# Fifteen gate pairs and two plain tiles, with the operand work moved ahead

## The chip, the cores and the metric

The kernel runs on one core of one Trainium2 chip. The metric is the device time of one execution in microseconds (us), as the median of several runs. One execution was also recorded by the hardware profiler; all rows shown below are from such a recording. Engines are named as in the profile: PE (TensorE matmuls), PEld (its weight loads), DVE (VectorE), ACT (ScalarE), POOL (GpSimd), SP (SyncE). SPq is SP's queue of DMA issues.

## The reference

One layer of a hybrid backbone is run for 512 latent tokens and for 128 context tokens. The kernel holds them together as 640 columns (T = 640). After a norm and a modulation the layer input h (1024 features) goes through one projection into four branches: a gated convolution (a), a bidirectional linear recurrence (b), attention (c), and a chunked gated MLP (d). Each branch gives an output y of 256 features. The four are joined under gates and projected, and a second half (norm, a convolutional feed-forward block) follows:

```python
g_a, g_b, g_c, g_d = jnp.split(jax.nn.sigmoid(h @ lw['w_gate'] + lw['b_gate']), N_BRANCH, axis=-1)
merged = (g_a * (y_a @ lw['w_br_a']) + g_b * (y_b @ lw['w_br_b'])
          + g_c * (y_c @ lw['w_br_c']) + g_d * (y_d @ lw['w_br_d']))
return merged @ lw['w_o'], kh, vh, s_f, s_b
```

The change lies in the stage that computes `merged`: for each of four branches, eight output tiles of 128 features, each a gate product (1024 features deep) and a branch product (256 deep).

## The kernel before

**Precision.** Every operand of a large product is kept as two parts: a high part (ACT copies it into the rounded type) and a low part (DVE subtracts the high part from the original). A product of a block takes three matmuls: high by high, high by low, low by high. All matmuls of this stage are 128 by 128 by 320; the 640 columns are two halves of 320 (HC = 320).

**Plain tiles.** `gate_tile` computes one output tile directly: 2 halves, 8 blocks of h, 3 matmuls each (line 375), then a sigmoid on ACT (line 1003), then 2 halves, 2 blocks of y, 3 matmuls each, then a product on DVE into `merged` (line 1014). For the plain tiles of branch d the low part of the weights is made by an ACT copy with scale -1 (line 151) and an accumulating DMA from POOL (`low_dma`).

**Pairs.** Two output tiles n and n + 4 of a branch form a pair. Weights and columns are cut in two by two blocks, and the pair is computed with seven block products in place of eight (`gprod` for h, line 1186; `bprod` for y, line 1195). Each of the seven takes 4 blocks of h and 1 of y, with 3 matmuls each. The price is sums and differences of blocks:

- of h, made once: three differences on DVE (line 1051), one sum (line 1071), and the high and low parts of the results (`g_split`, lines 1077 and 1078). Operands 7, 5 and 6 go to the regions F, X1 and X0; operand 3 is written over the block (0, 1) of h itself, in the tiles XH and XL. The generator `g_operands` does this while attention and the last projections run.
- of y, made once per branch: the plain y is loaded into the tile D (`y_load`: a DMA from SP for the high part, then an accumulating DMA from POOL for the low part), four sums on DVE (`y_sums`), and copies into the region C, and into y itself (`y_split`).
- of the weights, made for each pair: raw weights (two loads, line 1122; the second of an odd pair goes to region G), four sums (`g_s01`, `g_s23`), and the units A, B, C and Z (Z in region S0) with high and low parts (`g_a`, `g_al`, `g_b`, `g_c`, `g_zh`, `g_zl`). The units A, B, C take in turn the three places of the pool `w`, which the plain tiles use too, and every fourth unit takes region B.

The list `PAIRS` starts in branch d at n = NPL. With NPL = 2 the tiles 0, 1, 4, 5 of branch d are plain and fourteen pairs follow. `g_first` prepares pair 0; `g_all` runs the pairs. `g_pair` writes one pair: products 1, 2, 6, 5, 7, 4, 3, with the copies, sigmoids and weight units of the next pair written between them. Products 1, 6, 7 and 4 add up in one accumulator, b1; ACT copies it between (to `ga`, then `gb`).

**Order of the work.** A scheduler orders the instructions of each engine by its own simulation of when they are ready, with those that were written earlier first. `keep_in_program_order` pins an instruction behind the one that was written last on its engine. The wrappers `oact`, `ovec`, `opool` do that for every call while `fixed[0]` is true, which holds from the start of the pairs in `g_all`. Before that they are plain calls. `act` and `vec` in this part of the kernel are always plain.

Generators such as `g_operands` and `attn` are jobs: a running count of TensorE time, `now`, advances with the matmuls that are written, and a job is resumed when its next due time is reached (`yield 2` means 2 us later). `R` holds flags: "scores" is set one step after attention has written its last score products, "ya" when the convolution branch's y is split (line 676), "yc" when attention's y is written, "ada39" when the last of the early modulation columns is done; `drain` resumes jobs until a condition holds.

Of the kernel before, what the change touches and what calls it, by code (L numbers as in the profile page):

```python
# [9 lines left out]
F32 = mybir.dt.float32  # L10
F32R = mybir.dt.float32r
U8 = mybir.dt.uint8
AF = mybir.ActivationFunctionType
ALU = mybir.AluOpType
AX = mybir.AxisListType

P = 128
# [25 lines left out]
""".split()  # L43
WARM = 100
UE = [5, 3, 1]
NPL = 2
LOWD = ("ac", "ax", "ab", "d")
T = 640
TS = 512
HC = 320  # L50
# [20 lines left out]
def tile_step(ctx: ExitStack, tc: tile.TileContext, a: dict, outs: list, dbg=None):  # L71
    nc = tc.nc
# [7 lines left out]
    gp = ctx.enter_context(tc.tile_pool(name="gp", bufs=4))  # L80
# [15 lines left out]
    def step(j):  # L96
        try:
            j[0] = now[0] + (next(j[1]) or 0.0) * j[2]
        except StopIteration:
            jobs.remove(j)  # L100
# [14 lines left out]
    def drain(done):  # L115
        busy[0] = True
        while not done():
            assert jobs
            for j in list(jobs):
                step(j)  # L120
            now[0] += 1.0
        busy[0] = False
# [3 lines left out]
    def nm(s):  # L126
        cnt[0] += 1
        return f"{s}_{cnt[0]}"

    def region(tag, shape, dt=F32):  # L130
        return big.tile(shape, dt, tag=tag, name=nm(tag))
# [23 lines left out]
    ten, vec, pool = [Ordered(e, boot) for e in (nc.tensor, nc.vector, nc.gpsimd)]  # L155
    act, mm = Ordered(nc.scalar, boot).activation, ten.matmul
    ovec, opool, oact = Ordered(nc.vector), Ordered(nc.gpsimd), Ordered(nc.scalar).activation
# [51 lines left out]
    for x in LORD.split():  # L209
        if x[0] == "w":  # L210
            i, h = int(x[1]), int(x[2])
# [180 lines left out]
    R = {}  # L392
# [567 lines left out]
    for s in SECTIONS:  # L960
        for n in range(2):
            if s in TOK:
                plain(lambda s=s, n=n: rows(a["w_tok"][TOK.index(s), n], 4, 256),
                      lambda w, s=s, n=n: tok_tile(s, n, w))
            else:
                plain(lambda s=s, n=n: feat(a["w_in"][OFF[s] // P + n], dma=s in LOWD),
                      lambda w, s=s, n=n: in_tile(s, n, w))

    hdr = dram.tile([2, 2, P, 4, HC], F32, name="hdr")
# [19 lines left out]
    GI = dict(a=0, b=1, c=2, d=3)  # L989
    PAIRS = [(0, n) for n in range(NPL, 4)] + [(bi, n) for bi in range(1, 4) for n in range(4)]  # L990
    GPAIR = len(PAIRS)
# [44 lines left out]
    gx, gw = {}, {}  # L1036

    def g_operands():
        while "cg" not in R:
            yield 1  # L1040
        d, g = region("D", [P, 2, 4, HC]), region("G", [P, 4, HC])
        yield 8
        for x, h, c in ((d[:, 0], 0, 1), (d[:, 1], 1, 1), (g, 0, 0)):
            yield 10
            nc.sync.dma_start(x, hdr[h, c])
        while "ya" not in R:
            yield 1
        yield 5
        a21, a22, a11 = d[:, 0], d[:, 1], g
        for o, x, y in ((a22, a21, a22), (a21, a11, a21), (a11, a22, a11)):  # L1050
            tc.keep_in_program_order(vec.tensor_tensor(o, x, y, ALU.subtract))
            yield 2
        gx["x"] = {}
        for i, h, c in ((1, 0, 0), (2, 1, 0), (4, 1, 1), (3, 0, 1)):
            cs = slice(c * HC, (c + 1) * HC)
            gx["x"][i] = xh[:, 4 * h:4 * h + 4, cs], xl[h][:, :, cs]
        for i, x, t, key in ((7, a21, "F", "scores"), (5, a22, "X1", "yc"), (6, a11, "X0", "yc")):
            while key not in R:
                yield 1
            y = region(t, [P, 2, 4, HC], F32R)  # L1060
            gx["x"][i] = y[:, 0], y[:, 1]
            g_split(i, x)
            if i == 5:
                nc.sync.dma_start(a22, hdr[1, 0])
            yield 1.5
        gx["t3"] = a22, a11
        gx["Y"] = a21.rearrange("p a t -> p (a t)")
        gx["S"] = a22.rearrange("p a t -> p (a t)").rearrange("p (i k c) -> p i k c", i=2, k=5)
        y_load(0)
        yield 7  # L1070
        vec.tensor_tensor(a22, a22, a11, ALU.add)
        y_sums()
        R["gx3"] = True

    def g_split(i, x):
        h, l = gx["x"][i]
        act(h, x, AF.Copy)
        vec.tensor_tensor(l, x, h.bitcast(F32), ALU.subtract)

    def y_load(bi):  # L1080

        if bi < 2:
            h, l = [R["y" + BR[bi]][:, i].rearrange("p k t -> p (k t)").bitcast(F32) for i in range(2)]
        else:
            h, l = [(ybd if bi == 2 else ycd)[:, i].rearrange("p k t -> p (k t)") for i in range(2)]
        nc.sync.dma_start(gx["Y"], h)
        opool.dma_start(gx["Y"], l, accum_op=ALU.add)
# [25 lines left out]
    def gp_id(p_):  # L1113
        return PAIRS[p_]
# [16 lines left out]
    def low(w, x, h):  # L1131
        ovec.tensor_tensor(w, x, h.bitcast(F32), ALU.subtract)
# [5 lines left out]
    def g_al(p_, r):  # L1138
        w = gw[p_, "A"]
        low(w[:, 1], r[0], w[:, 0])  # L1140

    def g_s01(p_, r):

        s = gw[p_, "S"] = gx["S"] if p_ else region("G", [P, 2, 5, P])
        ovec.tensor_tensor(s[:, 0], r[0][:, 0], r[1][:, 1], ALU.add)
        ovec.tensor_tensor(s[:, 1], s[:, 0], r[1][:, 0], ALU.add)

    def g_s23(p_, r):
        s = gw[p_, "S"]
        b21, (b22, b12) = r[0][:, 1], (r[1][:, 0], r[1][:, 1])  # L1150
        ovec.tensor_tensor(b12, b12, b22, ALU.add)
        ovec.tensor_tensor(b21, s[:, 1], b21, ALU.add)

    def g_b(p_):
        s = gw[p_, "S"]
        b = gw[p_, "B"] = gunit(p_, 1)
        oact(b[:, 0], s, AF.Copy)
        low(b[:, 1], s, b[:, 0])

    def g_c(p_, r):  # L1160
        c = gw[p_, "C"] = gunit(p_, 2)
# [74 lines left out]
    def g_pair(p_, r):  # L1236
# [7 lines left out]
        bi, n0 = gp_id(p_)  # L1244
        new = n0 == (NPL if bi == 0 else 0)
        if new:
            gx["bi"] = bi
        if n0 == (NPL if bi == 0 else 0) + 1 and bi < 3:
            y_load(bi + 1)
# [68 lines left out]
        gprod(b2, p_, 3, False)  # L1318
        if n0 == (NPL if bi == 0 else 0) + 1 and bi < 3:
            y_sums()  # L1320
# [6 lines left out]
    def g_first(r):  # L1327
        drain(lambda: "ada39" in R)
        g_a(0, r[0])
        g_al(0, r[0])  # L1330
        g_s01(0, r[0])
        g_s23(0, r[0])
        g_b(0)
        for x in g_c(0, r[0]):
            low(*x)
        g_zh(0, r[0])
        return r

    def g_all(r):
        drain(lambda: "gx3" in R)  # L1340
        r[1] = gp_load(1)
        gx["C"] = region("C", [P, 2, 3, HC], F32R)
        fixed[0] = True
        sums_ = down_sums()
        for p_ in range(GPAIR + 1):
            for _ in range(4 if p_ else 0):
                next(sums_, None)
            if p_ == GPAIR:
                fixed[0] = False
                for j in range(GATES + 1, GATES + 3):  # L1350
                    ld[j] = units[j][0]()
                    rd[j] = units[j][1](ld[j])
            g_pair(p_, r)
        m_split(2)
        m_split(3)
# [1066 lines left out]
    for tok in BOOT:  # L2422
        name, on_act = tok.rstrip("."), tok[-1] == "."
        p = re.fullmatch(r"(m)(\d)(\d)([HL]+)|(tu|xo|sc|wh|wl)(\d)([ab])|([a-z]+)(\d+)|(\w+)", name).groups()
# [27 lines left out]
    ten, vec, pool, act, mm = nc.tensor, nc.vector, nc.gpsimd, nc.scalar.activation, nc.tensor.matmul  # L2452
# [111 lines left out]
```

## Time and profile before

| what | value |
|---|---|
| median of 3 runs | 1002.12 us (1001.3 to 1003.15) |
| the profiled execution's own time | 1001.64 us |
| its span, first to last instruction | 999.9 us |
| granted TensorE clock, mean | 0.998 of full speed |
| plain gate tiles in the trace | about 271.5 to 309.25 us |
| the fourteen pairs | 309.25 us to about 525 us |

A timeline row gives start (us), duration (us), engine, line, operation, out<-in by the program's names, shapes and count, and in brackets how long the engine was idle before it and what released it. Line 151 is the line of the wrapper, so instructions of the ordered calls are told apart by their tiles: `w`, `B`, `S` are weight units, `D` is y and the sums of weights, `C` the split sums of y, `ga` and `gb` the two gates of a pair, `F`, `X`, `XH`, `XL` the operands of h. On such rows a group of instructions of one kind is one row with its count. A row of the chain gives start, duration and engine with line. A row of DMA issues gives the queue, the size and the median time from issue to landing.

### The profile page before, as it was taken

The numbers are of one execution on the slowest core, as the hardware profiler recorded it, in microseconds if no ns is written. First come the engines' busy times: TensorE is split into PE (matmuls) and PEld (weight loads), VectorE is DVE, ScalarE is ACT, GpSimd is POOL, SyncE is SP. The second block draws the span as 40 slices with busy tenths as digits, with TensorE's granted clock in tenths as the row PEclk, the third lists the DMA queues.
The fourth block names the chain that finished last, engine by engine and source line by source line (L and its number), as shares of the span: only waits on it lengthen the run. The fifth ranks groups of instructions, "written<-read, shape, count | busy, mean of one in ns | idle before, by whom it ended". The sixth has DMA issues, their size and how long they took to land.

```text
span 999.9 us, 18964 instructions
## 1 busy us (share of the span) xinstructions
PE 987.3 (99%) x7467; PEld 935.7 (94%) x7467; DVE 860.6 (86%) x1411; ACT 585.3 (59%) x1009; POOL 169.9 (17%) x227
## 2 busy tenths in 40 slices
PE   8999999999999999999999999999999999999997
PEld 6899999999999999999998799999999999888886
DVE  6678899878677989898879978999999998999796
ACT  6642343445555565555655376777777777756672
POOL 1000020323110223233010021222222222100004
PEclk9999999999999999999999999999999999999999
DMA  9874343498475999999348785766666666976842
GB/s 357 331 252 155 123 143 119 132 251 255 107 212 188 309 235 237 291 257 293 106 163 319 296 316 161 216 161 173 177 168 163 177 171 192 365 257 226 283 127 105
DMA packets 71016, 214.16 MB, mean 214 GB/s; under 512 B 9744, under 2 KB 24880, under 8 KB 68240
## 3 DMA queue, kind: packets, MB, share of 16 engines
q1 hardware_dynamic: 43968, 151.22, 43.2%
q0 software_dynamic: 26960, 61.75, 26.8%
q8 instruction: 58, 0.95, 0.4%
q14 instruction: 30, 0.25, 0.1%
HBM read 168.62 MB, written 48.51 MB: 217 GB/s over the span
## 4 chain that ended last, share of the span: by engine, by line
PE 89%; DVE 5%; DMA 3%; issue 2%; POOL 1%; SPq 0%; ACT 0%; POOLq 0%; DVEq 0%; ACTq 0%
PE g L1622 21%; PE m L1186 17%; PE g L375 16%; PE m L2094 9%; PE m L1622 5%; PE g L2094 4%; PE g L1195 3%; PE g L948 2%; PE m L1392 1%; PE m L1195 1%; PE m L539 1%; PE m L1617 1%; DMA S<-in_w_ada_dram 1%; DMA B<-in_w_ada_dram 1%; PE g L151 1%
## 5 line engine op out<-in xcount | busy, mean ns | idle before, releaser
L375 PE MATMUL g<-XH,w 128*128 128x320 f32 x704 | 169.4, 316 | 0.0
L375 PEld LDWEIGHTS g<-XH,w 128*128 128x128 f32 x704 | 120.3, 188 | 2.5 <-issue 1.2
L375 PE MATMUL g<-XL,w 128*128 128x320 f32 x352 | 108.7, 309 | 0.0
L1186 PE MATMUL m<-XH,w 128*128 128x320 f32 x336 | 79.8, 309 | 0.0
L375 PEld LDWEIGHTS g<-XL,w 128*128 128x128 f32 x352 | 66.3, 188 | 0.0
L2094 PE MATMUL m<-w,XH 128*128 128x512 f32 x246 | 58.5, 390 | 0.0
L1186 PEld LDWEIGHTS m<-XH,w 128*128 128x128 f32 x336 | 57.6, 188 | 0.0
L2094 PEld LDWEIGHTS m<-w,XH 128*128 128x128 f32 x246 | 46.1, 188 | 9.5
L1186 PE MATMUL m<-XL,w 128*128 128x320 f32 x168 | 51.9, 309 | 0.0
L151 ACT ACTIVATE w<-raw 128x640 fp32r<-128x640 f32 (+3 forms) x53 | 49.6, 952 | 3.2 <-PE g L375 2.0
L151 DVE TENSOR_TENSOR w<-raw,w 128x640 fp32r<-128x640 f32 (+3 forms) x43 | 43.9, 1039 | 1.9 <-ACT w L151 1.9
L151 POOL DMA_DIRECT2D wsum<-in_w_dn_dram x36 | 37.4, 1256 | 44.6 <-issue 40.6
L1186 PE MATMUL m<-X,w 128*128 128x320 f32 x264 | 42.6, 309 | 0.0
L1186 PEld LDWEIGHTS m<-X,w 128*128 128x128 f32 x264 | 39.7, 188 | 0.0
L151 DVE SCALAR_TENSOR_TENSOR X<-MG,p2t,X 128x641 f32<-128x641 f32 x44 | 38.9, 883 | 0.9 <-ACT X L151 0.2
L151 DVE SCALAR_TENSOR_TENSOR X<-X,p2t,X 128x641 f32<-128x641 f32 x44 | 38.9, 884 | 0.9
L1622 PE MATMUL g<-XL,w 128*128 128x320 f32 x240 | 38.6, 310 | 0.0
L1622 PE MATMUL g<-XL,C 128*128 128x320 f32 x240 | 38.3, 309 | 0.0
L151 ACT ACTIVATE gb<-m 128x320 f32<-128x320 f32 x28 | 12.3, 438 | 43.0 <-PE m L1186 43.0
L1622 PEld LDWEIGHTS g<-XL,w 128*128 128x128 f32 x240 | 36.0, 188 | 0.6 <-ACT MG L151 0.3
L1622 PEld LDWEIGHTS g<-XL,C 128*128 128x128 f32 x240 | 36.0, 188 | 0.0
L1186 PEld LDWEIGHTS m<-XL,w 128*128 128x128 f32 x168 | 31.5, 188 | 0.0
(612 smaller groups left out, 2852.0 us busy)
## 6 DMA issues: line engine op xcount, KB each, us to landing
wsum<-in_w_dn_dram POOLq DMA_DIRECT2D x30, 512.0 KB, 11.0
raw<-in_w_up_dram SPq DMA_DIRECT2D x30, 512.0 KB, 5.1
raw<-in_w_gp_dram SPq DMA_DIRECT2D x21, 640.0 KB, 6.0
raw<-in_w_in_dram SPq DMA_DIRECT2D x19, 512.0 KB, 4.3
H<-in_w_adt_dram SPq DMA_DIRECT2D x19, 512.0 KB, 4.1
raw<-wsum SPq DMA_DIRECT2D x12, 512.0 KB, 5.9
actx<-X POOLq DMA_DIRECT2D x22, 256.0 KB, 4.7
wsum<-wsum POOLq DMA_DIRECT2D x10, 512.0 KB, 10.3
```

Source lines behind the costliest of these rows:

```text
L151: r = f(*args, **kw)
L375: mm(o, w[:, h, k0 + k, :], r(k)[:, s], start=(k == 0 and i == 0), stop=(k == kt - 1 and i == 2))
L539: mm(m[W * g:W * g + W, (i - s0) * W:(i - s0 + 1) * W], lhs, rhs, start=True, stop=True, tile_position=(64 * par, W * g))
L948: mm(o, x(kx)[:, ts], w[:, h, k, :], start=(kx == 0 and i == 0), stop=(kx == 7 and i == 2))
L1186: mm(o, w[:, h, n, k, :], x[:, k, :], start=(first and k == 0 and j == 0), stop=(k == 3 and j == 2), skip_group_check=True)
L1195: mm(o, w[:, h, n, 4, :], x[l], start=(first and j == 0), stop=(j == 2), skip_group_check=True)
L1392: mm(m, mh[MHN[q]][:, hx, k % 2, t * P:(t + 1) * P], wo[q][:, hw, k % 2, :], start=(k == 0 and i == 0), stop=(k == 7 and i == 2))
L1617: mm(o, w[:, k, :], x[:, k, :], start=(first and not part and k == 0 and j == 0), stop=(part == 1 and k == 3), skip_group_check=True)
L1622: z = mm(o, w[:, k, :], x[:, k, :], start=(first and k == 0 and j == 0), stop=(k == 3 and j == 2), skip_group_check=True)
L2094: mm(ps, s[t // 4][:, hx, k, o:o + P], w[:, hw, k, c0:c1], start=first, stop=i == 2 and bi == len(batch) - 1 and k == len(ks) - 1, skip_gr ...
```

## The change

NPL goes from 2 to 1, so only tiles 0 and 4 of branch d are plain and the pairs begin with (d, 1). The rest of the change moves the preparation:

- `g_operands` starts the three differences when "scores" and "ada39" are set, not 5 us after "ya". The block (1, 0) of h that the last sum needs is loaded into a tile of its own in region S0 before the differences, not into D after operand 5's split.
- `y_load(0)` is written behind the split of operand 7, not after all splits; the pause of 7 us after it goes.
- `g_split` calls `oact` and `ovec`, not `act` and `vec`.
- The sums S of pair 0 are two tiles of the pool `gt`, not one in region G, and B's high and low parts of pair 0 are made in two halves.
- All of pair 0's preparation behind unit A moves from `g_first` to the start of `g_all`, behind the wait for "gx3".

```diff
-NPL = 2
+NPL = 1
...
-        while "ya" not in R:
+        while "scores" not in R or "ada39" not in R:
             yield 1
-        yield 5
+        a12 = region("S0", [P, 4, HC])
+        nc.sync.dma_start(a12, hdr[1, 0])
         a21, a22, a11 = d[:, 0], d[:, 1], g
         for o, x, y in ((a22, a21, a22), (a21, a11, a21), (a11, a22, a11)):
             tc.keep_in_program_order(vec.tensor_tensor(o, x, y, ALU.subtract))
...
             g_split(i, x)
-            if i == 5:
-                nc.sync.dma_start(a22, hdr[1, 0])
+            if i == 7:
+                gx["Y"] = a21.rearrange("p a t -> p (a t)")
+                y_load(0)
             yield 1.5
         gx["t3"] = a22, a11
-        gx["Y"] = a21.rearrange("p a t -> p (a t)")
         gx["S"] = a22.rearrange("p a t -> p (a t)").rearrange("p (i k c) -> p i k c", i=2, k=5)
-        y_load(0)
-        yield 7
-        vec.tensor_tensor(a22, a22, a11, ALU.add)
+        vec.tensor_tensor(a22, a12, a11, ALU.add)
         y_sums()
         R["gx3"] = True

     def g_split(i, x):
         h, l = gx["x"][i]
-        act(h, x, AF.Copy)
-        vec.tensor_tensor(l, x, h.bitcast(F32), ALU.subtract)
+        oact(h, x, AF.Copy)
+        ovec.tensor_tensor(l, x, h.bitcast(F32), ALU.subtract)
...
-        s = gw[p_, "S"] = gx["S"] if p_ else region("G", [P, 2, 5, P])
-        ovec.tensor_tensor(s[:, 0], r[0][:, 0], r[1][:, 1], ALU.add)
-        ovec.tensor_tensor(s[:, 1], s[:, 0], r[1][:, 0], ALU.add)
+        s = gw[p_, "S"] = [gx["S"][:, i] if p_ else gp.tile([P, 5, P], F32, tag="gt", name=nm("s"))
+                           for i in range(2)]
+        ovec.tensor_tensor(s[0], r[0][:, 0], r[1][:, 1], ALU.add)
+        ovec.tensor_tensor(s[1], s[0], r[1][:, 0], ALU.add)
...
-        oact(b[:, 0], s, AF.Copy)
-        low(b[:, 1], s, b[:, 0])
+        for x, h, l in ((gx["S"], b[:, 0], b[:, 1]),) if p_ else [(s[i], b[:, 0, i], b[:, 1, i]) for i in range(2)]:
+            oact(h, x, AF.Copy)
+            low(l, x, h)
...
         g_a(0, r[0])
         g_al(0, r[0])
+        return r
+
+    def g_all(r):
+        drain(lambda: "gx3" in R)
         g_s01(0, r[0])
         g_s23(0, r[0])
         g_b(0)
         for x in g_c(0, r[0]):
             low(*x)
         g_zh(0, r[0])
-        return r
-
-    def g_all(r):
-        drain(lambda: "gx3" in R)
         r[1] = gp_load(1)
```

More of the change, by code (lines that the diff above doesn't have):

```diff
@@ L1151, in g_s23 @@
         ovec.tensor_tensor(b12, b12, b22, ALU.add)
-        ovec.tensor_tensor(b21, s[:, 1], b21, ALU.add)
+        ovec.tensor_tensor(b21, s[1], b21, ALU.add)
     def g_b(p_):
```

## The prediction

> **What bounds the kernel now.** I read the page's engine line first, then the chain that ended last, then that chain's pieces around the place of the change, then the timelines of ScalarE, VectorE, SyncE and GpSimd there.
>
> ```profile
> PE 987.3 (99%) x7467; PEld 935.7 (94%) x7467; DVE 860.6 (86%) x1411; ACT 585.3 (59%) x1009; POOL 169.9 (17%) x227
> PE 89%; DVE 5%; DMA 3%; issue 2%; POOL 1%; SPq 0%; ACT 0%; POOLq 0%; DVEq 0%; ACTq 0%
> ...
> 282.38 27.04 PE g L375 x183
> 309.41 1.76 PE m L1186 x12
> 311.17 0.44 PE g L1195 x3
> ```
>
> TensorE is the bound: 99% busy, 89% of the chain. From 282.38 on the chain is TensorE alone: 183 matmuls of plain tiles, then the pairs. Twelve matmuls of 320 columns take 1.76 us, 0.1467 us each. So what counts is the number of matmuls, and whether any of them comes to wait.
>
> ```profile
> 291.65:309.25 17.60, 17.60 (x122) 17.60 (x121) 11.12 (x14) 6.16 (x6) 2.98 (x5) 1.00 0.79 227
> 309.25:324.65 15.40, 15.40 (x107) 15.40 (x106) 12.53 (x18) 10.30 (x18) 0.00 (x0) 1.00 0.40 129
> 324.65:340.05 15.40, 15.40 (x107) 15.40 (x106) 14.46 (x22) 8.84 (x14) 2.99 (x5) 1.00 0.96 298
> ```
>
> These stretches (busy time and instructions of PE, PEld, DVE, ACT, POOL) are the last two plain tiles, pair 0 and pair 1. A plain tile has 60 matmuls (2 halves, 8+2 blocks, 3 products each), two have 120: 17.60 us. A pair has 7 products of 15, so 105: 15.40 us, that is 105 times 0.1467 with nothing left over. No pair waits now.
>
> **The change part by part.**
>
> (1) Two plain tiles go, a pair comes: 120 matmuls less 105, 15 times 0.1467 = **-2.20 us**. The weights moved stay at 1,280 KB. The first pair then starts at 291.65, where the third plain tile starts now, instead of at 309.25. Whatever prepares it has 17.60 us less.
>
> (2) Weight places. Units A, B and C of pair 0 take the three `w` slots in turn, each when the plain tile before it lets go.
>
> ```profile
> 291.85 1.28 ACT L151 ACTIVATE w<-raw 128x1280 fp32r<-128x1280 f32 x1 [0.96 <-PE g L375]
> 300.70 1.27 ACT L151 ACTIVATE w<-G 128x1280 fp32r<-128x1280 f32 x1 [1.01 <-PE g L375]
> 309.50 1.37 ACT L151 ACTIVATE w<-raw 128x640 fp32r<-128x640 f32 x2 [1.01 <-PE g L375]
> ```
>
> A, B and C were copied right behind the ends of the second, third and fourth plain tile. With two tiles fewer, A's place comes free when the last tile of ab ends (271.5, by the row at 271.59 below), B's when the first plain tile ends (291.65 - 8.80 = 282.85), C's at 291.65. Against the pair's start all three keep at least the distance they have now, so I cost this at nothing. S of pair 0 moves from region G to two `gt` tiles, which lets its four sums run early, and lets G be refilled for pair 1 when the last sum of h has read it instead of after B's low part. The fourth operand's block loads into S0, which by the code is given up with ada39, so the load that had to wait for D no longer stands in the SP queue behind the store of yc. The two ScalarE copies and GpSimd accumulations for the low parts of the two dropped tiles go as well; neither was on the chain. All of this: 0, covered by TensorE; without that cover it would show as the rival on operands below.
>
> (3) The split of the fourth operand. `g_split` now goes through the ordered calls, and inside the pairs that pins it. Before, it ran ahead:
>
> ```profile
> 305.93 1.28 ACT L1077 ACTIVATE XH<-D 128x1280 fp32r<-128x1280 f32 x1 [3.96 <-PE g L375]
> ...
> 311.21 0.44 ACT L151 ACTIVATE ga<-m 128x320 f32<-128x320 f32 x1 [0.34 <-PE m L1186]
> 311.71 0.42 ACT L151 ACTIVATE g<-g 128x320 f32<-128x320 f32 x1
> 312.04 1.27 ACT L151 ACTIVATE B<-raw 128x1280 fp32r<-128x1280 f32 x1
> 313.21 1.08 ACT L151 ACTIVATE C<-D 128x640 fp32r<-128x640 f32 x2
> 314.19 0.56 ACT L151 ACTIVATE ga<-ga,cst 128x320 f32<-128x320 f32 x1
> 315.17 0.44 ACT L151 ACTIVATE gb<-m 128x320 f32<-128x320 f32 x1 [0.42 <-PE m L1186]
> ...
> 308.19 1.49 DVE L1078 TENSOR_TENSOR XL<-D,XH 128x1280 fp32r<-128x1280 f32 x1
> ...
> 313.48 0.49 DVE L151 TENSOR_TENSOR ga<-m,ga 128x320 f32<-128x320 f32 x1 [0.87 <-PE m L1186]
> 313.97 0.82 DVE L151 TENSOR_TENSOR D<-raw,G 128x640 f32<-128x640 f32 x1
> ...
> 319.60 0.49 DVE L151 TENSOR_TENSOR gb<-m,gb 128x320 f32<-128x320 f32 x1
> ...
> 317.17 1.92 PE L1186 MATMUL m<-F,S 128*128 128x320 f32 x12
> ```
>
> I count from the pair's start. In the written order ScalarE now does: ga (1.96), g, B, the two copies of C (3.96 to 4.94), the split's high part (4.94 to 6.21), and only then ga's sigmoid. VectorE does the split's low part from about 6.25 to 7.74 (1.49 as above), then ga's sum, 7.66 to 8.15 (next starts overlap by 0.08), which now stands behind it. The sigmoid follows at 8.2 and the copy of gb about 0.45 later, ending near 9.1. Product 7 (tile F,S) writes the same accumulator that gb is copied from; its place is 317.17 - 309.25 = 7.92. It would start near 9.2: **+1.3 us**, from 7.92 to between 9.1 and 9.3. Lower bound 0, if the pin does not put the split there. Behind that, VectorE's sums, the low parts of C and of A and the next sums keep their spacing of 6.12 us from ga's sum to the subtraction of gb (313.48 to 319.60): 7.66 + 6.12 + 0.49 = 14.27, against product 3, which writes that bank, at 12.76 + 1.28 = 14.04: **+0.25 us**.
>
> (4) The sums of y. Everything on ScalarE from the copies of C on waits for them.
>
> ```profile
> 283.05 0.33 SPq L905 DMA_DIRECT2D ycd<-C  x1
> 286.59 0.52 SPq L1086 DMA_DIRECT2D D<-E  x1
> ...
> 296.18 0.87 POOL L151 DMA_DIRECT2D D<-E  x1 [8.83 <-DMA D<-E]
> ...
> 304.07 2.07 DVE L151 TENSOR_TENSOR D<-D 128x320 f32<-128x320 f32 x4 [6.35 <-DMA D<-E]
> ...
> 309.59 0.82 DVE L1014 TENSOR_TENSOR MG<-g,gt 128x640 f32<-128x640 f32 x1
> 310.32 1.55 DVE L151 TENSOR_TENSOR w<-raw,w 128x640 fp32r<-128x640 f32 x2
> 311.79 0.82 DVE L151 TENSOR_TENSOR S<-raw,S 128x640 fp32r<-128x640 f32 x1
> ...
> D<-E SPq DMA_DIRECT2D x1, 640.0 KB, 9.0
> D<-A SPq DMA_DIRECT2D x1, 640.0 KB, 3.4
> ```
>
> Now y is asked for at 286.59 and is there at 304.07, 17.5 us later: 9.0 for the plain load behind the store of yc (and, by the code, the reload of D with the block of h), 0.6 to the next issue, 7.9 for the accumulation. That was 5 us before the pair. When is it asked for after the change? The differences come behind the last scores:
>
> ```profile
> 270.40 0.29 DVE L886 TENSOR_TENSOR C<-m,C 128x128 fp32r<-128x128 f32 x1 [0.90 <-ACT C L885]
> 271.59 0.82 DVE L436 TENSOR_TENSOR MG<-g,MG 128x640 f32<-128x640 f32 x1 [0.90 <-PE g L375]
> 274.06 1.49 DVE L676 TENSOR_TENSOR A<-MG,A 128x1280 fp32r<-128x1280 f32 x1 [1.64 <-ACT A L675]
> ...
> 277.11 1.48 DVE L1051 TENSOR_TENSOR D<-D 128x1280 f32<-128x1280 f32 x1
> ...
> 267.65 0.42 DVE L859 TENSOR_SCALAR X<-X,ast 128x384 f32<-128x384 f32 x1
> 274.92 0.82 PE L862 MATMUL m<-cst,X 128*128 128x128 f32 x6
> ```
>
> The first difference can follow the row at 270.40, so it starts near 270.7. The second is written 2 us of schedule later, which falls behind the split of ya (274.06), and A's low part (1.49) also wants VectorE there: it starts near 275.9 and ends at 277.4. The third difference, the split of operand 5, a copy and the split of operand 7 follow; that makes 281.5 for the request (280.5 at best). The plain load now stands ahead of the stores of yc in the SP queue, so I take 4.0, near the 3.4 of D<-A; then 0.5, and 7.9 for the accumulation, whose competitors (yc's store, pair 1's load, wsum) are as many as before: y at about 293.5. VectorE's list from there to the split's low part: the four sums 2.0, a merge 0.73, C's two low parts 1.47 (starts 309.59, 310.32, 311.79), Z's 0.75, together 4.95, so 298.45 against the 297.9 (291.65 + 6.25) used above: **+0.55 us**. Bounds: 0 for y before 292.9; with the old 17.5 us, y comes at 299.0 and the term is 6.05.
>
> What else is queued: GpSimd's accumulation waits for the plain load, and behind it stand only the sums for the down projection, needed far later. SP's queue holds pair loads that are early now. Attention shares VectorE with the moved differences (three of 1.48, 4.5 us). Its last scaling ended at 268.07 and TensorE used it at 274.92, so 6.9 us cover them; beyond that the first plain tile's matmuls would wait.
>
> Sum: -2.20 + 1.30 + 0.25 + 0.55 = **-0.10 us**. The profiled execution took 1001.64 (span 999.9 and 1.74 around it), 0.48 below the median of 1002.12. So 1001.54 on its scale, and **1002.0** as a median.
>
> One rule bears on this. The Trainium skill, "Perfetto Trace Analysis", section "Identifying Performance Opportunities", says that one generally gains by improving the most contended engine. That engine is TensorE here, and by this rule the whole 2.20 us would be gained. The ordered ScalarE and VectorE rows of pair 0 speak against it, and I weigh it as the first rival.
>
> **The rivals.**
>
> *Nothing waits.* The split is done early enough, or the chain in (3) has slack that I do not see, and y is there by 292.9. Then the time is 1002.12 - 2.20 = 999.9. For it: in pair 0 ScalarE was busy only 10.30 of 15.40, and no pair waited before. Against: the pinned order, row by row. This is what the rule above gives.
>
> *y comes late* (the other side). Place: ScalarE's copies of C and all behind them. Price: 1 us for each us of y after 292.9, on top of 1.55. It decides from 293.55 on, where -2.20 is used up; from 295.6 on it is slower by over 0.2%; at 299.0 it gives 1002.12 - 2.20 + 1.55 + 6.05 = 1007.5. For it: the accumulation took 7.9 before, and VectorE may put other work ahead of operand 7's split. Against: the plain load is freed of the queue that made it 9.0.
>
> *Operands of pair 0 late on VectorE.* From 270.4 to 295.6, where product 6 starts (27 matmuls into the pair), VectorE has ten instructions of about 1.49 (three differences, the low parts of three operands, ya, A and B, the last sum of h) and six of 0.82 (four sums, two products), 19.8 us in 25.2; if the scheduler places y's wait ahead of B's low part or fills other gaps less well, I put it at up to the four sums, 3.3 us more: 1002.0 + 3.3 = 1005.3. Against: two of the sums need nothing but weights and can run early.
>
> *The change does not save on TensorE.* Were VectorE (14.46 of 15.40 in pair 1) to bind, a pair would cost no less than two tiles. Each of the 14 pairs is 15.40, so I give this nothing of its own.
>
> **How the numbers follow.** Measurement tells about 0.2%, 2.0 us. Forecast (stall of 1.3 to 2.8 us, 1001.2 to 1002.8): 0.52. Nothing waits: 0.15. y late by more than 2 us: 0.20. Operands late: 0.13, a quarter of it inside 0.2%. Faster 0.15, same 0.55, slower 0.30. The range 999.8 to 1005.2 takes in the first two cases and the nearer half of the others.
>
> **What would show it.** Right: pair 0 starts near 291.7; in it product 7 (F,S) starts 9 to 10 us after the pair's start, held by ScalarE's copy of gb, and the split (XH<-D) stands on ScalarE between the copies of C and ga's sigmoid; later pairs are 15.40; the whole gate stage ends within 0.5 us of before. Wrong: XH<-D ahead of the pair, or product 7 at 7.9; y's sums after 296; a wait at product 6 for B or X; or a change in the stages behind the gates, which I take as shifted whole.

## The result and the profile after

Changed kernel: **1006.29 us** median of 5 runs (1005.7 to 1008.38); kernel before, beside it: 1002.54 us (1001.3 to 1003.15). The ratio is 1.0043, 95% interval 1.0028 to 1.0057: slower by 0.4%, with an interval that lies wholly above 1, and outside the range 999.8 to 1005.2. The profiled execution took 1006.04 us with a span of 1004.2.

The engine line and the chain by engine, from the profile page of the changed kernel:

```profile
PE 987.3 (98%) x7452; PEld 935.0 (93%) x7452; DVE 869.5 (87%) x1425; ACT 587.2 (58%) x1018; POOL 168.3 (17%) x225
...
PE 88%; DVE 5%; DMA 4%; issue 1%; POOL 1%; ACT 1%; SPq 0%; POOLq 0%; DVEq 0%; ACTq 0%
```

The fifteen matmuls are gone (7467 to 7452), yet PE's busy time is the same 987.3 us: some of the rest ran slower (the last section says why). Where, the stretches of time show (length, then busy time and count of PE, PEld, DVE, ACT, POOL; granted clock; DMA share; GB/s): the last two plain tiles, pair 0, what is left of the disturbance, a later pair.

```profile
273.76:291.36 17.60, 17.60 (x134) 16.89 (x133) 11.84 (x12) 7.38 (x10) 2.98 (x5) 1.00 0.51 147
291.36:313.61 22.25, 18.51 (x107) 17.64 (x106) 18.55 (x26) 12.74 (x22) 0.00 (x0) 0.85 0.50 186
313.61:329.14 15.53, 15.53 (x108) 15.53 (x107) 15.29 (x23) 9.27 (x15) 5.07 (x9) 1.00 0.87 276
329.14:344.54 15.40, 15.40 (x108) 15.40 (x106) 12.34 (x18) 8.90 (x15) 0.00 (x0) 1.00 0.69 258
```

Pair 0 starts at 291.36, and takes 22.25 us in place of 15.40. All else is as forecast: no wait before it, later pairs of 15.40, and product 4 of the last pair starts at 524.67 in place of 520.20, 4.47 later, which the span shows again (4.3). The two rows of the chain, after and before:

```profile
524.67 1.64 PE m L1187 x12
```

```profile
520.20 1.76 PE m L1186 x12
```

So the whole loss is in pair 0. The timeline there, engine by engine:

```profile
248.73 20.11 SPq L1121 DMA_DIRECT2D raw<-in_w_gp_dram  x3
...
280.40 0.52 SPq L1085 DMA_DIRECT2D D<-E  x1
283.53 0.33 SPq L905 DMA_DIRECT2D ycd<-C  x1
...
284.20 0.87 POOL L151 DMA_DIRECT2D D<-E  x1 [20.03 <-DMA D<-E]
...
284.15 1.48 DVE L151 TENSOR_TENSOR X<-G,X 128x1280 fp32r<-128x1280 f32 x1
293.14 1.54 DVE L151 TENSOR_TENSOR D<-D 128x320 f32<-128x320 f32 x3 [7.51 <-DMA D<-E]
294.61 0.82 DVE L151 TENSOR_TENSOR s<-raw,raw 128x640 f32<-128x640 f32 x1
...
297.94 0.82 DVE L151 TENSOR_TENSOR raw<-s,raw 128x640 f32<-128x640 f32 x1
298.68 1.55 DVE L151 TENSOR_TENSOR w<-s,w 128x640 fp32r<-128x640 f32 x2
...
303.43 1.49 DVE L151 TENSOR_TENSOR XL<-D,XH 128x1280 fp32r<-128x1280 f32 x1 [0.99 <-ACT XH L151]
...
298.06 0.74 ACT L151 ACTIVATE S<-raw 128x640 fp32r<-128x640 f32 x1 [0.61 <-DVE raw L151]
298.70 0.42 ACT L151 ACTIVATE ga<-m 128x320 f32<-128x320 f32 x1
...
291.36 0.31 PE L1187 MATMUL m<-XH,w 128*128 128x320 f32 x1
...
299.17 0.90 PE L1187 MATMUL m<-X,w 128*128 128x320 f32 x2 [3.69 <-ACT ga L151]
...
300.56 2.87 PE L1187 MATMUL m<-X,w 128*128 128x320 f32 x10
...
306.93 1.92 PE L1187 MATMUL m<-F,S 128*128 128x320 f32 x12
...
321.66 1.92 PE L1187 MATMUL m<-F,S 128*128 128x320 f32 x12
```

VectorE stands still for 7.51 us until y has landed. Only then come the four weight sums of pair 0 (first and last of them: 294.61 and 297.94) and B's low parts, though three weight loads were issued from 248.73 on, pair 0's two among them (in e11 below both have landed by 259.9). ScalarE's queue is in order too: the copy of Z (S<-raw) needs the third sum, and the copy of ga, which only needs TensorE, stands behind it at 298.70. TensorE waits 3.69 us for that copy, at product 6 (m<-X,w). A wait at product 6 was one of the prediction's signs of being wrong, there for B or X; here it is the copy of ga that ends last. Then the pinned split and ga's sum hold product 7 (F,S) until 306.93, 15.57 after the pair's start.

I call *stall* the time that pair 0 loses: the start of product 7 of pair 1 (the row at 321.66), less the start of pair 0, less 15.40 + 7.92 (the spacing before). Here 321.66 - 291.36 - 23.32 = **6.98 us**, where the prediction had summed 2.10.

### The profile page after: what moved, and what is told of

It reads as the page before. It is cut to its first block, busy times and chain, and to the rows that moved or that the text cites. A ratio compares the mean times of both kernels' runs of the same rounds, so it can differ in the third digit from the quotient of the medians.

```text
span 1004.2 us, 18954 instructions
## 1 busy us (share of the span) xinstructions
PE 987.3 (98%) x7452; PEld 935.0 (93%) x7452; DVE 869.5 (87%) x1425; ACT 587.2 (58%) x1018; POOL 168.3 (17%) x225
## 4 chain that ended last, share of the span: by engine, by line
PE 88%; DVE 5%; DMA 4%; issue 1%; POOL 1%; ACT 1%; SPq 0%; POOLq 0%; DVEq 0%; ACTq 0%
PE g L1623 21%; PE m L1187 18%; PE g L375 12%; PE m L2095 9%; PE m L1623 5%; PE g L2095 4%; PE g L1196 3%; PE g L948 2%; PE m L1393 2%; PE m L151 2%; PE g L151 1%; PE m L1196 1%; DMA D<-E 1%; PE m L539 1%; PE m L1618 1%
## 5 line engine op out<-in xcount | busy, mean ns | idle before, releaser
L375 PE MATMUL g<-XH,w 128*128 128x320 f32 x640 | 155.0, 317 | 0.0
L375 PEld LDWEIGHTS g<-XH,w 128*128 128x128 f32 x640 | 109.5, 188 | 2.5 <-issue 1.2
L375 PE MATMUL g<-XL,w 128*128 128x320 f32 x320 | 98.8, 309 | 0.0
L1187 PE MATMUL m<-XH,w 128*128 128x320 f32 x368 | 87.4, 309 | 0.0
L1187 PEld LDWEIGHTS m<-XH,w 128*128 128x128 f32 x368 | 63.2, 188 | 0.2 <-ACT gb L151 0.2
L375 PEld LDWEIGHTS g<-XL,w 128*128 128x128 f32 x320 | 60.3, 188 | 0.0
L1187 PE MATMUL m<-XL,w 128*128 128x320 f32 x184 | 56.9, 309 | 0.0
L1187 PE MATMUL m<-X,w 128*128 128x320 f32 x264 | 45.2, 320 | 3.7 <-ACT ga L151 3.7
L151 DVE TENSOR_TENSOR w<-raw,w 128x640 fp32r<-128x640 f32 (+3 forms) x46 | 46.9, 1037 | 0.9 <-ACT w L151 0.8
L1623 PE MATMUL g<-XL,w 128*128 128x320 f32 x240 | 38.6, 310 | 0.0
L1623 PEld LDWEIGHTS g<-XL,w 128*128 128x128 f32 x240 | 36.0, 188 | 0.6 <-ACT MG L151 0.3
L1187 PEld LDWEIGHTS m<-XL,w 128*128 128x128 f32 x184 | 34.5, 188 | 0.0
## 6 DMA issues: line engine op xcount, KB each, us to landing
wsum<-in_w_dn_dram POOLq DMA_DIRECT2D x30, 512.0 KB, 11.9
```

The costliest lines, as they stand in the source:

```text
L151: r = f(*args, **kw)
L375: mm(o, w[:, h, k0 + k, :], r(k)[:, s], start=(k == 0 and i == 0), stop=(k == kt - 1 and i == 2))
L1187: mm(o, w[:, h, n, k, :], x[:, k, :], start=(first and k == 0 and j == 0), stop=(k == 3 and j == 2), skip_group_check=True)
L1623: z = mm(o, w[:, k, :], x[:, k, :], start=(first and k == 0 and j == 0), stop=(k == 3 and j == 2), skip_group_check=True)
```

## The experiments

Two theories at first. *Order*: the sums stand behind the wait for y in VectorE's fixed order; put them elsewhere and the stall goes. *Pin* or *load*: the pinned split is the cause, or VectorE and the transfers are full whatever the order. All runs, each with the kernel before beside it on the same chip (5 or 11 runs of each; the difference of medians; the shift of product 4 of the last pair against the 520.20 of before, as the gate stage's end; stall as above, both from one profiled execution):

| kernel | median us | ratio to before (95%) | difference | gate end | stall |
|---|---|---|---|---|---|
| changed | 1006.29 | 1.0043 (1.0028-1.0057) | +3.75 | +4.47 | 6.98 |
| e11 sums with operand 7 | 1003.05 | 1.0011 (1.0002-1.002) | +1.09 | +0.23 | 0.92 |
| e2 split free | 1006.78 | 1.0047 (1.0034-1.006) | +4.82 | +4.44 | 6.89 |
| e3 high part of y only | 1000.83 | 0.9991 (0.9982-1.0) | -1.13 | -1.18 | 1.48 |
| e4 before, split pinned | 1002.45 | 1.0007 (0.9998-1.0016) | +0.49 | +0.37 | 0.92 |
| e13 sums behind differences | 1006.1 | 1.0044 (1.0032-1.0057) | +4.55 | +4.20 | new wait |
| e14 y on VectorE | 1000.53 | 0.9989 (0.998-0.9997) | -1.02 | -1.11 | 1.47 |
| e15 the same, split free | 999.91 | 0.9986 (0.9977-0.9994) | -1.64 | -2.48 | 0.28 |
| e16 e13, split free | 1007.32 | 1.0057 (1.0043-1.0071) | +5.77 | +4.62 | new wait |
| e18 sums behind operand 6 | 1000.97 | 0.9992 (0.9983-1.0001) | -0.76 | -1.52 | 1.12 |
| e19 the same, split free | 1001.25 | 0.9996 (0.9988-1.0005) | -0.48 | -0.06 | 1.61 |
| e6 changed, fourteen pairs | 1003.43 | 1.0017 (1.0008-1.0026) | +1.70 | +1.28 | 1.47 |
| e7 other transfers later | 1006.23 | 1.0045 (1.0033-1.0058) | +4.50 | +4.55 | 7.07 |

The gate's end in one trace and the difference of medians agree within 1.2 us. In e13 and e16 part of pair 0 ran ahead of the last plain tile, so the stall can't be read as elsewhere; they have a wait of their own, told below.

**e11, the sums written earlier.**

```diff
             if i == 7:
                 gx["Y"] = a21.rearrange("p a t -> p (a t)")
                 y_load(0)
+                g_s01(0, ld[GATES][0])
+                g_s23(0, ld[GATES][0])
+                g_b(0)
...
     def g_all(r):
         drain(lambda: "gx3" in R)
-        g_s01(0, r[0])
-        g_s23(0, r[0])
-        g_b(0)
```

> Edit: in the changed kernel the four weight sums of pair 0 and the split of their result (unit B) are written behind the request for y, inside the fourth operand's loop, instead of behind the sums of y; all else as changed. Theory (order): pair 0 lost 6.85 us because VectorE's fixed order put these sums behind the wait for y (idle 7.51 us to 293.14, then sums 294.61 to 298.7), while their weights had landed long before. Then VectorE now does the sums and B's low part (about 4 x 0.74 + 2 x 0.73 = 4.4 us) within that wait, what is left behind y is the y sums, a merge, C, Z and the split, and the stall falls to about 2.1 us, what the prediction had summed for the split and y: 4 to 5 us under the changed kernel, 1001.5 to 1002.5 in the units of the runs so far. Rival (load): VectorE or the transfers are simply too full ahead of pair 0, and the order does not matter: the stall only moves, gain under 1 us. Rival (pin): the pinned split of the fourth operand is most of the stall: gain 1 to 2 us at most.

The stall fell to 0.92, but pair 0 started 1.80 later, at 293.16. The scheduler put the first sum into the middle of attention, where its weights had not come. VectorE's timeline:

```profile
257.01 0.29 DVE L886 TENSOR_TENSOR C<-m,C 128x128 fp32r<-128x128 f32 x1 [0.90 <-ACT C L885]
259.91 0.83 DVE L151 TENSOR_TENSOR s<-raw,raw 128x640 f32<-128x640 f32 x1 [2.61 <-DMA raw<-in_w_gp_dram]
260.65 1.02 DVE L849 TENSOR_TENSOR X<-m,B 128x384 f32<-128x384 f32 x2
```

The same kind of mistake, a wait ahead of work that could run, in another place. Of the stall 6.06 us went, and 1.80 of it was lost again ahead of the pair. Part of the fall comes from this delay itself, since y was ready 0.41 us behind the pair's start and not 1.78. The run speaks for the order theory, against load, and against the pin as the main cause.

**e2, the split unpinned.**

```diff
-        oact(h, x, AF.Copy)
-        ovec.tensor_tensor(l, x, h.bitcast(F32), ALU.subtract)
+        act(h, x, AF.Copy)
+        vec.tensor_tensor(l, x, h.bitcast(F32), ALU.subtract)
```

> Edit: in the changed kernel the split of the operands goes back to the unordered calls, as it was before the change; all else as changed. Theory (order): the sums still stand behind the wait for y, so most of the 6.85 us stays; the split's low part (1.49 us) now may run anywhere behind y, between the sums of y, which takes ga's sigmoid out from behind it but pushes the weight sums back by its 1.49: between 1.5 us faster and 1 us slower than the changed kernel. Rival (pin): the pinned split makes the stall: 3 to 5 us faster. Rival (load): no change within 0.5 us.

6.89: the split went to the front of VectorE's list, and the weight sums by so much to the back. Pin is out as the main cause; between order and load this run does not decide.

**e3, y without its low part.**

```diff
         nc.sync.dma_start(gx["Y"], h)
-        opool.dma_start(gx["Y"], l, accum_op=ALU.add)
+        if bi:
+            opool.dma_start(gx["Y"], l, accum_op=ALU.add)
```

> Edit: the changed kernel without the accumulation of y's low part for the first block of the gates (that part of y is left out; its 640 KB are not moved). Theory (order): y is there at about 283.6 instead of 293.1, so the wait of 7.51 us at the sums of y is gone, and all that stands behind it comes before the pair starts; what remains is the pinned split, which still stands behind the copies of C, and these wait for a matmul tile's end at 291.4: stall 0 to 1.5 us, 5 to 7 us faster than the changed kernel. Rival (load): VectorE is full anyway: the stall falls by less than 3 us. Rival (pin): the wait for y costs little, the pin stays: less than 3 us faster.

The sums of y ran at 285.39 and the weight sums at 287.37, in the same order as in the changed kernel, and 5.5 us of the stall went. So the wait and the order together make it; either cures it.

**e4, the kernel before with the split pinned**: the diff of e2 the other way round.

> Edit: the kernel before (fourteen pairs, four plain tiles) with the split of the operands in the ordered calls, as in the change; nothing else. Prediction's step 3 alone: in pair 0 the split's high part stands behind the copies of C and its low part ahead of ga's sum, so the seventh product starts at about 9.2 instead of 7.92 us behind the pair's start, and the third at most 0.25 later: 1.3 to 1.55 us slower than before. Rival (the pin costs nothing): the split is done in ScalarE's and VectorE's idle time before the pair, since y is there 5 us before it: no change within 0.3 us. Rival (pin is the main cause): 3 us slower or more.

Step 3 alone. ScalarE's, VectorE's and TensorE's rows:

```profile
312.67 1.08 ACT L151 ACTIVATE C<-D 128x640 fp32r<-128x640 f32 x2
313.65 1.26 ACT L151 ACTIVATE XH<-D 128x1280 fp32r<-128x1280 f32 x1
316.87 0.56 ACT L151 ACTIVATE ga<-ga,cst 128x320 f32<-128x320 f32 x1 [1.96 <-DVE ga L151]
...
314.94 1.49 DVE L151 TENSOR_TENSOR XL<-D,XH 128x1280 fp32r<-128x1280 f32 x1 [2.92 <-ACT XH L151]
...
317.81 2.03 PE L1186 MATMUL m<-F,S 128*128 128x320 f32 x12
```

The pair started at 308.71, so product 7 comes at 9.10 (predicted 9.2, in place of 7.92), in the order of rows that the prediction wrote down. At the end of the pair 0.92 is left of it. In the runs, 0.07%, it can't be told from nothing.

**e13, the sums in the gap, first try**: e11, and the first three sums pinned behind the three differences.

> Edit: as in e11, but the first three weight sums of pair 0 are also kept in program order behind the three differences of h, so that they can't stand ahead of attention; y as in the changed kernel. In e11 the first of them stood in VectorE's order ahead of a block of attention, waited there 2.61 us for its weights, and pair 0 started 1.80 us later than in the changed kernel (293.16 against 291.36), while its stall fell from 6.98 to 0.92. Theory (order): the pair starts at 291.4 again, y is there at about 293.1 as in the changed kernel, and VectorE's list behind it is the sums of y 1.99, a merge 0.73, C 1.47, Z 0.75 and the split 1.40, so product 7 comes about 2.5 us late: stall 2.3 to 2.9 us, 4 to 4.7 us under the changed kernel's gate stage, about 1002 to 1002.5 in all, no better than e11. Rival (load): VectorE has no room there: the three sums and B's low part push the request for y or the last scores back, and the stall stays above 4.

My theory missed here, by 4 us. The pin put the sums ahead of attention's last output (VectorE's row `C<-m,C`), which came at 287.19 in place of 283.22, and yc is stored behind that. The chain of waits, and ScalarE's row:

```profile
287.28 0.21 DVE C L886
...
287.50 11.93 DMA ycd<-C
...
299.54 1.10 ACT C L151 x2
```

```profile
299.54 1.10 ACT L151 ACTIVATE C<-D 128x640 fp32r<-128x640 f32 x2 [1.80 <-DMA ycd<-C]
```

Region C is free for y's copies only when yc's store has read it, and the store took 11.9 us where it took 4.7 in the changed kernel. Weight transfers ran beside it; that they slowed it was not tried. So the sums did push attention's end back, much as the rival had it, but what came late by it was the store of yc; the sums of y ran at 290.31 already.

**e16**, e13 with the split unpinned:

> Edit: as e13, and the split of the operands in the unordered calls; y by the DMAs as in the changed kernel. Theory: with the sums out of the way, the split's low part comes right behind the sums of y (at about 295.1) and ga's sum no longer waits for it; product 7 is on time or less than 0.5 us late, what stands behind (C, Z) costs up to 1 us: stall 0 to 1.2 us, about 1000 to 1001, faster than before. Rival (y late decides whatever the order): y comes at 293.1 against a start at 291.4, stall above 2 us.

Also missed: now VectorE waited 6.33 us, until 302.11, for pair 1's load into G, which SP issues behind that store.

**e18, the sums in the gap, second try.**

```diff
+        z = ovec.tensor_tensor(l, x, h.bitcast(F32), ALU.subtract)
+        if i == 6:
+            tc.keep_in_program_order(z)
...
+        g_s01(0, ld[GATES][0])
+        g_s23(0, ld[GATES][0])
+        g_b(0)
         gx["t3"] = a22, a11
```

The three calls in `g_all` go, and the first three sums are pinned as in e13, now behind the split of operand 6.

> Edit: in the changed kernel the four weight sums of pair 0 and the split of unit B are written behind the operands' loop, and the first three sums are pinned behind the split of operand 6, so that on VectorE they stand in the gap of 7.51 us before y and ahead of nothing that attention or the store of yc needs; split of the fourth operand pinned, y by the DMAs, as in the changed kernel. Theory (order): start 291.4 and y at about 293.1 as in the changed kernel; behind y only the sums of y 1.99, a merge 0.73, C 1.47, Z 0.75 and the split, so its low part starts at about 298.1, product 7 at about 301: stall 1.5 to 2.2 us instead of 6.98, total about 1001 to 1001.7, 4.5 to 5.5 us under the changed kernel. Rival (y's lateness itself, not what is queued behind it): stall above 4 us. Rival (transfers): as in e13 something else of that stretch comes late in its place, the store of yc or the load for pair 1: stall above 4 us.

This is the clean test: same start (291.23), same arrival of y (293.00), same pin, only the place of the sums differs. VectorE's timeline:

```profile
284.02 1.48 DVE L151 TENSOR_TENSOR X<-G,X 128x1280 fp32r<-128x1280 f32 x1
285.42 0.82 DVE L151 TENSOR_TENSOR s<-raw,raw 128x640 f32<-128x640 f32 x1
...
288.49 1.56 DVE L151 TENSOR_TENSOR w<-s,w 128x640 fp32r<-128x640 f32 x2
293.00 1.02 DVE L151 TENSOR_TENSOR D<-D 128x320 f32<-128x320 f32 x2 [2.95 <-DMA D<-E]
...
297.68 1.49 DVE L151 TENSOR_TENSOR XL<-D,XH 128x1280 fp32r<-128x1280 f32 x1
299.08 0.48 DVE L151 TENSOR_TENSOR ga<-m,ga 128x320 f32<-128x320 f32 x1
```

TensorE's rows for the stall, the start of pair 0 and product 7 of pair 1:

```profile
291.23 0.31 PE L1194 MATMUL m<-XH,w 128*128 128x320 f32 x1
...
315.67 1.92 PE L1194 MATMUL m<-F,S 128*128 128x320 f32 x12
```

The gap of 7.51 us is now filled with 4.6 us of sums and B's low parts, 2.95 of it are left, and the stall is 1.12. So **5.86 of the 6.98 us are the order**; pin, lateness of y and the rest of the list together make 1.12. That split is read from one trace of each kernel. In the medians, each against the kernel before, the two lie 4.51 us apart, where the gate's ends lie 5.99 apart.

**e19**, e18 with the split unpinned:

> Edit: as e18, with the split of the operands in the unordered calls as before the change. Theory (order, pin as the rest): what e18 still stalls is the pinned split behind the late y; unpinned it comes right behind the first sums of y and leaves only ga's sum at the end of VectorE's list (at about 299): stall 0.5 to 1.5 us, 0.5 to 1 us under e18. Rival: y at 293.1 sets the end of the same list either way: no difference of more than 0.3 us to e18.

Missed: 1.61, no gain. The split's low part now stood between the sums of y, ScalarE's copies of C waited for the last of these (1.17 us), and ga's sum came at 299.61, 0.53 later than in e18, where the pair had started 0.65 earlier: nearly the same place in the pair. Product 7 started 9.18 behind the pair's start, in e18 9.31. But in e18 TensorE had six matmuls of later products to do ahead of product 7, and here it stood still for 1.09 us.

**e14 and e15, y without DMAs.**

```diff
+        if not bi:
+            vec.tensor_tensor(gx["Y"], h, l, ALU.add)
+            return
         nc.sync.dma_start(gx["Y"], h)
         opool.dma_start(gx["Y"], l, accum_op=ALU.add)
```

For this branch both parts of y lie in SBUF, so one VectorE instruction of 1.49 us does the work of 12 us of transfers. e15 also unpins the split.

> Edit: in the changed kernel the first block's y is put together on VectorE in one instruction (high plus low part, both in SBUF) in place of the load and the accumulation by DMA; order and pinned split as in the changed kernel. Theory (order): nothing on VectorE waits for a transfer there any more, so the weight sums run ahead of the pair at no cost of order; the stall is that of the pinned split alone, 0.9 to 1.5 us (e4 and e3 showed 0.92 and 1.48): 5.5 to 6 us faster than the changed kernel, about 1000.8. Rival (load): the 1.49 us more on VectorE push the sums behind the pair's start: stall 2 to 4 us.

> Edit: as e14, and the split of the operands in the unordered calls, as before the change. Theory: nothing of pair 0 waits any more, it takes 15.40 us, and the whole 2.20 us of the fifteen matmuls are gained against the kernel before (the prediction's rival of no wait): about 999.8, 0.2% under before. Rival: the copies of C, which wait for the last plain tile, or VectorE's list keep a stall of 0.5 to 2 us whatever the split: 1000.3 to 1002.

The stalls came near what was expected, 1.47 and 0.28; the medians gained less, 4.77 us on the changed kernel for e14 (5.5 to 6 expected), 1.64 on the kernel before for e15 (2.20 expected). e15's stretches of pair 0 and pair 1:

```profile
291.11:306.79 15.68, 15.68 (x108) 15.41 (x106) 14.78 (x21) 11.72 (x21) 0.00 (x0) 1.00 0.28 84
306.79:322.19 15.40, 15.40 (x108) 15.40 (x106) 15.16 (x23) 9.25 (x15) 5.00 (x9) 1.00 0.89 277
```

Nearly nothing waits (0.28), at a VectorE load 1.49 us higher than in the changed kernel: rival load is out for good. e15 is the fastest version, 0.14% under the kernel before. That is less than the 0.2% that the prediction took as the least that can be told, but the interval, 0.9977 to 0.9994, excludes 1. In e14 and e15 GpSimd also issued four transfers for the down projection at 259.7 already, as its queue was free; e18 reached nearly the same without that.

**e6, the change without the fifteenth pair**: NPL = 2 in the changed kernel.

> Edit: the changed kernel with fourteen pairs and four plain tiles again, all its other parts as changed (weight sums in places of their own, early differences and y, pinned split). Theory (distance): y comes 16 us before the pair starts, so the sums that stand behind it cost nothing; what is left is the pinned split, 0.9 us as in e4: within 1 us of the kernel before, 1001.5 to 1003. Rival (the other parts cost by themselves, by VectorE's load or the moved transfers): 2 us or more above before.

Stall 1.47, 1.70 us above before, more than I expected: the pin's 0.92 and 0.55 more, with the fourth sum and B's low parts still late: they stand on VectorE at 310.02 to 312, behind the merge of the last plain tile and behind the pair's start at 309.01. e3 and e14, which keep the changed kernel's order and have y early, show the same row order there and the same 1.48 and 1.47. So the other parts of the change lose some by themselves, but what made it 6.98 is that y comes 1.8 us behind the pair's start and not 16 us ahead.

**e7, the down projection's transfers later**: in `g_all`, `4 if p_ else 0` becomes `4 if p_ > 1 else 0`.

> Edit: in the changed kernel the first four transfers for the down projection (512 KB each), which GpSimd issues right behind the accumulation of y, start a pair later; all else as changed. In the changed kernel y's plain load took 3.2 us and the accumulation of the same 640 KB 8.9, in e13, with the store of yc 4 us later, 6.3. Theory (contention): the accumulation falls to 4 to 7 us and y comes 2 to 5 us sooner; the list behind y is as long, but part of it falls ahead of the pair: stall 2 to 5 instead of 6.98. Rival (the accumulation is slow by itself or through the store of yc, which shares its time in both): y within 1 us of 293.1 and the stall within 1 us of 6.98.

The theory of contention by these transfers falls. The DMA view of e7, then of e13, for 278 to 300 and 278 to 306 us (count, size, us to landing):

```profile
ycd<-C SPq DMA_DIRECT2D x1, 1280.0 KB, 4.6
D<-E SPq DMA_DIRECT2D x1, 640.0 KB, 3.2
D<-E POOLq DMA_DIRECT2D x1, 640.0 KB, 9.1
```

```profile
ycd<-C SPq DMA_DIRECT2D x1, 1280.0 KB, 11.9
raw<-in_w_gp_dram SPq DMA_DIRECT2D x2, 640.0 KB, 7.0
D<-E SPq DMA_DIRECT2D x1, 640.0 KB, 3.2
D<-E POOLq DMA_DIRECT2D x1, 640.0 KB, 6.3
```

Without the four transfers the accumulation takes 9.1 us (8.9 with them); with the store of yc and pair 1's load some 4 us later it takes 6.3. Store and load were moved together, so which of them it is stays open.

## Why the prediction was wrong

- **Step 1, TensorE's work: right.** -2.20 us, pair 0 at 291.36 (291.65 predicted, 0.29 earlier by what comes before), later pairs 15.40. In e15, where little waits, the gate stage ends 2.48 earlier: 2.20 plus a start 0.54 earlier, less 0.28. The rule of the Trainium skill that the prediction weighed as its first rival comes out there in the trace, and in the changed kernel it does not: what counted was who waits.
- **Step 2, weight places: this failed.** It said that S in tiles of its own "lets its four sums run early", at cost 0. Free places and landed weights let them; the order did not. They were written behind the flag that y's sums set, and VectorE's queue runs in order, so they stood behind a wait of 7.51 us. This made 5.86 us (changed against e18).
- **The rival "operands of pair 0 late on VectorE" was the true case, and mis-sized**: chance 0.13, "up to the four sums, 3.3 us more". Its mechanism, y's wait ahead of other work, was right; its "against" (two sums can run early) was the error of step 2 again. The price was short because not the sums alone waited. B's low parts, 1.47 us, stood behind them on VectorE, ahead of C's and Z's, which step 4 had counted; and on ScalarE the copy of ga, for which TensorE waits, stood behind Z's copy. The split's low part, planned 6.25 us into the pair, started 12.07 into it (303.43), in e18 6.45.
- **Step 3, the pinned split: right in the mechanism.** Product 7 at 9.10 against 9.2 in e4; 0.92 for the pair against 1.30 + 0.25. The 0.25 at product 3 did not show.
- **Step 4, y: right in the arrival, partly by luck.** Asked for at 280.40 (281.5), plain load 3.2 (4.0), accumulation 8.9 (7.9), there at 293.14 (293.5): the request and the load were sooner, the accumulation longer. The prediction's own terms, 281.5, 4.0, 0.5 and 7.9, add up to 293.9 and not 293.5, which would have made its 0.55 into 0.95. The price of 0.55 belongs to a list without the weight sums; with them out of the way, pin and y together cost 1.12 where steps 3 and 4 had 2.10.
- **Attention and the stages behind: right.** No wait of TensorE ahead of pair 0; the later stages shift whole in the span. In every run with fifteen pairs the chain leaves TensorE behind the gate stage for a load of 8.4 to 9.0 us (XL<-in_w_up_dram, 8.71 from 526.32 on in the changed kernel), which is not on the chain of before. TensorE waits 1.4 us near it (0.6 before), but the shift stays: near 850 us the transfer C<-actp is issued 4.57 us later than before (854.72 against 850.15).

The prediction's sum, then, is about that of e18, whose difference to before (-0.76 in the medians) lies within 0.7 us of the -0.10 that it gave. This is no proof of its terms: in the trace e18's gate stage ends 1.52 us before that of the kernel before, since steps 3 and 4 were 0.98 too dear and pair 0 started 0.42 earlier.

## What to carry to other kernels

A free slot and a landed operand don't make an instruction early: read its place in its engine's order, and list what would stand behind each wait if that wait were a few us longer than the planner believes. When a wait is moved close to where its result is used, price everything queued behind it on that engine, and the in-order queues that this feeds, not the late instruction alone. And before transfers are rescheduled, ask whether they are needed: one 1.49 us instruction in place of two DMAs removed the wait that all this was about.

## What was not expected of the hardware

**The clock.** In the changed kernel TensorE's granted clock was also halved around the wait of 3.69 us. That is why fewer matmuls were busy for the same 987.3 us: the 107 of pair 0's stretch took 18.51 us and not the 15.70 that 0.1467 each would make. The stretches around it:

```profile
295.48:299.17 3.69, 0.00 (x1) 0.00 (x0) 3.69 (x6) 3.08 (x6) 0.00 (x0) 0.86 0.86 350
299.17:301.00 1.83, 1.78 (x5) 1.38 (x6) 1.83 (x4) 1.83 (x3) 0.00 (x0) 0.50 0.02 9
301.00:303.00 2.00, 2.00 (x10) 2.00 (x9) 1.44 (x2) 2.00 (x4) 0.00 (x0) 0.50 0.43 108
303.00:305.00 2.00, 2.00 (x9) 2.00 (x9) 1.57 (x2) 0.40 (x1) 0.00 (x0) 0.52 0.85 292
305.00:307.00 2.00, 2.00 (x16) 2.00 (x15) 1.97 (x4) 0.89 (x2) 0.00 (x0) 1.00 0.61 248
```

The clock was at 0.50 from 298.1, 2.6 us into the wait, until 304.9, 5.8 us after work had begun again, so product 6 and part of product 5 took up to twice as long (row 300.56: 10 matmuls in 2.87). It cost little here, since the copy of gb that product 7 needs ended only at 306.25 and product 7 started at 306.93: at most 0.7 us. In e13 product 7 itself ran at half clock, 3.57 us for its 12 matmuls in place of 1.92, on the path. The stretch at half clock was 6.8 us long in each of the five runs that have one (changed, e2, e7, e13, e16), whatever the wait. The Trainium skill, "TensorE: Matmul & The Clock Gate", Part 1, says that the clock is halved after an idle window of about 3.4 us and restored after a busy one of as long, and that these windows run freely and do not start with the kernel. The halves agree, and 6.8 us is two such windows, with TensorE idle for part of the first in each of the five runs. What does not agree is the idle time that it takes: in e2 a wait of 2.02 us was enough, the clock was 0.52 right behind it. Waits of 1.1 us (e19) and 1.3 us (e11) left it at 1.00.

**The accumulating transfer.** 640 KB within SBUF took 3.2 us as a plain load from SP's queue and 6.3 to 9.1 us as an accumulation from GpSimd's. In e7 it took 9.1 although GpSimd's other transfers were out of the way.

**A wait behind the gate stage.** In the profiled executions of e2, e11 and e15 the chain held a transfer of 5.1 to 6.6 us (C<-actp, near 850 us) that is not on the chain of before or of the changed kernel, and TensorE waited 0.4, 1.9 and 0.7 us behind it. e15's span is 1.5 us under before where its gate stage ends 2.48 earlier. Why it is there in some and not in others was not tried.
